# RoPE projection on one core: buffer counts, VectorE block transposes in three of four pairs, and a tail of eight single tiles

## The chip, the cores and the metric

The kernel runs on one core of one Trainium2 chip. The metric is the time of one execution on the device, in microseconds (us). The profile measures a span, from the first to the last instruction of the core; what lies around the span belongs to the time and not to the span.

## The reference

A batch of 16 sequences of 512 rows and 768 columns is multiplied by a 768 x 768 weight, and each of the 12 heads of 64 columns is rotated by its row's cosine and sine:

```python
y = np.matmul(x, weight).reshape(batch, seq, n_heads, head_dim)
y1, y2 = y[..., :32], y[..., 32:]
out1 = y1 * cos1 - y2 * sin1
out2 = y2 * cos2 + y1 * sin2
out = np.concatenate([out1, out2], axis=-1)   # float32, 16 x 512 x 768
```

## The kernel before

The 8192 rows are cut into 64 tiles of 128 rows, and the tiles into 32 pairs `n` of two tiles `s` = 0, 1 (two batches, the same rows `r`). This text numbers the tiles 2n+s, so tile 50 is the first of pair 25. A tile goes through six steps:

1. Load: `load` fetches it in one DMA of 384 KB on SP's queue into `xs` (10 buffers in `xpool`). `load_blocks` fetches a tile that `by_blocks` names in four DMAs of 96 KB into `xb` (`bpool`), each into 32 partitions with pieces of 768 bytes; the two DMAs to partitions 0 to 63 are issued by SP, the two to partitions 64 to 127 by ScalarE (ACT).
2. `cast`: ACT casts it to fp16 (`xc`, 6 buffers).
3. `transpose`: TensorE (PE) transposes it in six instructions into PSUM (`pt`, 2 buffers) and ACT copies that to `xT` (`tpool`, 9 buffers). A block tile is turned by `transpose_blocks` instead: one VectorE (DVE) instruction that transposes 32 x 32 blocks, from `xc` to `xT`.
4. `mm`: twelve matmuls into PSUM (`psy`, two buffers of three banks, a pair each).
5. `rope_pair`: DVE multiplies the pair by cosines and by sines in one instruction (`rope`, `tq`), GpSimd (POOL) adds the two halves (`add`, `ov`, 6 buffers).
6. `store`: ACT's queue writes the pair in one DMA of 768 KB, three pairs later.

The order on every engine is the program's. In the loop over the pairs, PE computes tile 2n+s, and then `upto("turn", ...)` and `upto("cast", ...)` turn and cast the tiles that are due: tile k+2 and tile k+4 after tile k in the steady part, and more from the point where the lookahead in `upto` grows, up to four tiles more, so that all transposes are done before the last `ALONE` pairs. The tiles of those pairs take their PSUM banks one by one, some of them from `pt`, and are rotated and added one by one (`rope_alone`, `add`); the very last is split between DVE and POOL (`rope_last`). `rope_pair` of the pair ahead of them runs in two halves. `load_plain(n + 5)` stands at the head of iteration n and `load_blocks(n + AHEAD_B)` at its end. Pairs 7, 9, ..., 27 have a block tile: 11 tiles. `by_blocks` and `upto` are

```python
def by_blocks(n, s):
    return s == 1 and n % 2 == 1 and 6 < n < NP - ALONE

def upto(what, k):
    k += min(4, max(0, k - 41) // 4)
```

Of the kernel before, what the change touches and what calls it, by code (L numbers as in the profile page):

```python
# [17 lines left out]
def kernel(  # L18
# [9 lines left out]
    nc = tc.nc  # L28
    P = nc.NUM_PARTITIONS

    B, S, H = x.shape
# [7 lines left out]
    NP = B * SB // 2  # L39
    CHUNKS = [(t, e) for t in range(NT) for e in range(2)]  # L40
    AHEAD = 7
    AHEAD_B = 4
    ALONE = 3

# [1 line left out]
    def where(n, s):  # L48
        return 2 * (n // SB) + s, n % SB

    def by_blocks(n, s):
        return s == 1 and n % 2 == 1 and 6 < n < NP - ALONE

    konst = ctx.enter_context(tc.tile_pool(name="konst", bufs=1))
    ident = konst.tile([P, P], FP16)
# [3 lines left out]
    w_raw = konst.tile([P, NT, 2, H], FP32)  # L59
    w_sb = konst.tile([P, NT, 2, H], FP16)  # L60

    xpool = ctx.enter_context(tc.tile_pool(name="xpool", bufs=10))
    bpool = ctx.enter_context(tc.tile_pool(name="bpool", bufs=AHEAD_B + 1))
    cpool = ctx.enter_context(tc.tile_pool(name="cpool", bufs=6))
    tpool = ctx.enter_context(tc.tile_pool(name="tpool", bufs=9))
    rpool = ctx.enter_context(tc.tile_pool(name="rpool", bufs=3))
    opool = ctx.enter_context(tc.tile_pool(name="opool", bufs=6))
    pt_pool = ctx.enter_context(tc.tile_pool(name="pt", bufs=2, space=bass.MemoryType.PSUM))
# [3 lines left out]
    xss, x16, xTT, psys, tqs, ovs = {}, {}, {}, {}, {}, {}  # L72
# [14 lines left out]
    def load_plain(n):  # L87
        for s in (0, 1):
            if n < NP and not by_blocks(n, s):
                load(n, s)  # L90


    def load_blocks(n):
        if n >= NP or not by_blocks(n, 1):
            return
        b, r = where(n, 1)
        xss[n, 1] = bpool.tile([P, H], FP32, tag="xb", name="xb")
        src = x[b].rearrange("(j a r) (q k) -> r q a j k", r=SB, a=R, q=NQ)
        dst = xss[n, 1].rearrange("p (j k) -> p j k", j=NQ)
        for q in (0, 2, 1, 3):  # L100
            eng = nc.sync if q < 2 else nc.scalar
            eng.dma_start(out=dst[ts(q, R)], in_=src[r, q])  # L102
# [9 lines left out]
    def cast(n, s, eng):  # L112
        xc = cpool.tile([P, H], FP16, tag="xc", name="xc")
        x16[n, s] = xc
        src = xss.pop((n, s))
        if by_blocks(n, s):
            src = src.rearrange("p (j a t e) -> p t (j a) e", j=NQ, t=NT, e=2)
        else:
            src = src.rearrange("p (m t e) -> p t m e", t=NT, e=2)
        copy(eng, xc.rearrange("p (t m e) -> p t m e", t=NT, e=2), src)  # L120

    def transpose(n, s, eng):
        xc = x16.pop((n, s)).rearrange("p (t m e) -> p t e m", t=NT, e=2)
        pt = pt_pool.tile([P, NT, 2, P], FP16, tag="pt", name="pt")
        for t, e in CHUNKS:
            nc.tensor.transpose(pt[:, t, e, :], xc[:, t, e, :], ident)  # L126
        xT = tpool.tile([P, NT, 2, P], FP16, tag="xT", name="xT")
        copy(eng, xT, pt)
        xTT[n, s] = xT

    def transpose_blocks(n, s):
        xT = tpool.tile([P, NT, P, 2], FP16, tag="xT", name="xT")
        nc.vector.transpose(  # L133
            out=xT.bitcast(FP32).rearrange("p t m e -> p (t m e)"),
            in_=x16.pop((n, s)).bitcast(FP32),
        )
        xTT[n, s] = xT.rearrange("p t m e -> p t e m")
# [5 lines left out]
    def psum(n, s):  # L143
        if n < NP - ALONE:
            if n not in psys:
                psys[n] = py_pool.tile([P, 3, 512], FP32, tag="psy", name="psy")
                if n < 2:
                    nc.tensor.matmul(  # L148
                        psys[n][:, 1], cold[:, 0:P], cold, start=True, stop=False
                    )  # L150
            cut = 512 if s == 0 else 256
            return [
                (psys[n][:, s, ds(s * 256, cut)], 0, cut, n < 2 and s == 1),
                (psys[n][:, s + 1, 0 : H - cut], cut, H, n < 2 and s == 0),
            ]
        if (n, s) not in psys:
            if (2 * (n - NP + ALONE) + s) % 3 == 1:
                psys[n, s] = [
                    pt_pool.tile([P, 512], FP32, tag="pt", name="psz") for _ in (0, 1)
                ]  # L160
            else:
                ps = py_pool.tile([P, 3, 512], FP32, tag="psy", name="psy")
                psys[n, s] = [ps[:, 0], ps[:, 1]]
        lo, hi = psys[n, s]
        return [(lo, 0, 512, False), (hi[:, 0 : H - 512], 512, H, False)]

    def mm(n, s, t, e):
        for ps, lo, hi, joined in psum(n, s):
            nc.tensor.matmul(  # L169
                ps,  # L170
                xTT[n, s][:, t, e, :],
                w_sb[:, t, e, lo:hi],
                start=((t, e) == CHUNKS[0] and not joined),
                stop=((t, e) == CHUNKS[-1] and not (joined and s == 0)),
            )

    def rope(n, c0, c1, ps):
        r = n % SB
        nh = (c1 - c0) // D
        if n not in tqs:  # L180
            tqs[n] = rpool.tile([P, 2, 2 * H], FP32, tag="tq", name="tq")
            ovs[n] = opool.tile([P, 2 * H], FP32, tag="ov", name="ov")
        nc.vector.tensor_tensor(  # L183
            out=tqs[n][:, :, c0:c1].rearrange("p j (h d) -> p j h d", d=D),
            in0=ps.rearrange("p (h d) -> p h d", d=D)
            .unsqueeze(1).broadcast_to((P, 2, nh, D)),
            in1=csn[:, :, r, :].unsqueeze(2).broadcast_to((P, 2, nh, D)),
            op=MULT,
        )

    def add(n, c0, c1, eng):
        w = c1 - c0
        tq = tqs[n][:, :, ds(c0, w)]
        eng.tensor_tensor(  # L194
            out=ovs[n][:, ds(c0, w)].rearrange("p (h t d) -> p h t d", t=2, d=HD),
            in0=tq[:, 0].rearrange("p (h t d) -> p h t d", t=2, d=HD),
            in1=tq[:, 1].rearrange("p (h t d) -> p h t d", t=2, d=HD)[:, :, ::-1, :],
            op=ADD,
        )

    def rope_pair(n, step=2 * H):
        ps = psys[n].rearrange("p b n -> p (b n)")
        for c in range(0, 2 * H, step):
            rope(n, c, c + step, ps[:, ds(c, step)])
            add(n, c, c + step, nc.gpsimd)

    def rope_alone(n, s):
        for ps, lo, hi, _ in psum(n, s):
            rope(n, s * H + lo, s * H + hi, ps)
# [25 lines left out]
    def store(n, eng, c0=0, c1=2 * H):  # L235
        b, r = where(n, 0)
        dst = out.rearrange("b (p r) h -> r p b h", r=SB)[r, :, b : b + 2]
        src = ovs[n].rearrange("p (b h) -> p b h", b=2)
        if c1 - c0 < 2 * H:
            s = c0 // H  # L240
            dst = dst[:, s, c0 - s * H : c1 - s * H]
            src = src[:, s, c0 - s * H : c1 - s * H]
        eng.dma_start(out=dst, in_=src)
# [21 lines left out]
    done = {"cast": 4, "turn": 4}  # L265

    def upto(what, k):
        k += min(4, max(0, k - 41) // 4)
        while done[what] < min(k, 2 * NP):
            n, s = divmod(done[what], 2)  # L270
            done[what] += 1
            if what == "cast":
                cast(n, s, nc.scalar)
            elif not by_blocks(n, s):
                transpose(n, s, nc.scalar)
# [13 lines left out]
    for k, c in enumerate(CHUNKS):  # L289
# [8 lines left out]
        out=csn[:, 1, :, HD:D], in0=sin_sb[:, :, 0:HD], scalar1=-1.0  # L298
    )
    rope_pair(0)  # L300
    upto("cast", 6)
    mm(1, 0, *CHUNKS[-1])
    upto("turn", 5)
    for c in CHUNKS:
        mm(1, 1, *c)
    upto("cast", 7)
    upto("turn", 6)
    upto("cast", 8)
    rope_pair(1)

    for n in range(2, NP):
        load_plain(n + AHEAD - 2)
        if n + 1 < NP and by_blocks(n + 1, 1):
            transpose_blocks(n + 1, 1)
        for s in (0, 1):
            for c in CHUNKS:
                mm(n, s, *c)
            upto("turn", 2 * n + s + 3)
            upto("cast", 2 * n + s + 5)
            if n >= NP - ALONE:  # L320
                if (n, s) != (NP - 1, 1):
                    rope_alone(n, s)
                    add(n, s * H, (s + 1) * H, nc.gpsimd)
        if n >= 3:
            store(n - 3, nc.scalar)
        load_blocks(n + AHEAD_B)
        if n < NP - ALONE:
            rope_pair(n, 2 * H if n < NP - ALONE - 1 else H)
    store(NP - 3, nc.scalar)
    store(NP - 2, nc.scalar)  # L330
    store(NP - 1, nc.scalar, 0, H)
    rope_last(NP - 1, 1)


# [33 lines left out]
```

## Time and profile before

| | |
|---|---|
| time, median of 5 runs | 163.8 us (163.66 to 164.43) |
| profiled execution: its own time | 165.71 us |
| profiled execution: its span | 163.9 us |
| PE busy | 150.3 us (92%) |
| DVE, POOL, ACT busy | 120.8, 110.2, 91.1 us |
| DMA | 53.17 MB, mean 324 GB/s |
| chain that ended last | PE 59%, DMA 18%, DVE 6%, POOL 5%, ACT 4% |

The profile is of one execution, whose time was 1.9 us over the median. A group's row gives its count, its busy time, the mean duration of one in ns, and the idle time of the engine before it with what ended that. PE's matmuls are pipelined, so the pitch from one group to the next in the chain of waits says more than the duration of one. In the DMA line, 9 means that the core's DMA engines were 90% or more busy.

### The profile page before, as it was taken

The numbers are of one execution on the slowest core, as the hardware profiler recorded it, in microseconds if no ns is written. First come the engines' busy times: TensorE is split into PE (matmuls) and PEld (weight loads), VectorE is DVE, ScalarE is ACT, GpSimd is POOL, SyncE is SP. The second block draws the span as 40 slices with busy tenths as digits, with TensorE's granted clock in tenths as the row PEclk, the third lists the DMA queues.
The fourth block names the chain that finished last, engine by engine and source line by source line (L and its number), as shares of the span: only waits on it lengthen the run. The fifth ranks groups of instructions, "written<-read, shape, count | busy, mean of one in ns | idle before, by whom it ended". The sixth has DMA issues, their size and how long they took to land.

```text
span 163.9 us, 2775 instructions
## 1 busy us (share of the span) xinstructions
PE 150.3 (92%) x1104; PEld 94.7 (58%) x1104; DVE 120.8 (74%) x68; ACT 91.1 (56%) x114; POOL 110.2 (67%) x40
## 2 busy tenths in 40 slices
PE   7899999999699999999999999999969799999910
PEld 2355666666366666666666666666646466666500
DVE  0556976788848787888878787879695757879970
ACT  3441866774566566765665657776193898610000
POOL 0000397777885787878788787877866774699990
PEclk9999999999999999999999999999999999999995
DMA  4999999999999999999999999999988445449766
GB/s 158 340 412 392 407 397 306 392 342 296 384 364 316 402 330 412 315 401 335 409 328 403 321 402 329 376 359 359 286 331 249 194 192 196 192 191 393 286 242 233
DMA packets 24141, 53.17 MB, mean 324 GB/s; under 512 B 2368, under 2 KB 8384, under 8 KB 24128
## 3 DMA queue, kind: packets, MB, share of 16 engines
q1 hardware_dynamic: 12096, 25.89, 47.9%
q10 hardware_dynamic: 12032, 27.10, 43.3%
q8 instruction: 8, 0.13, 0.3%
q14 instruction: 5, 0.04, 0.1%
HBM read 27.82 MB, written 25.17 MB: 323 GB/s over the span
## 4 chain that ended last, share of the span: by engine, by line
PE 59%; DMA 18%; DVE 6%; POOL 5%; ACT 4%; issue 2%; POOLq 1%; SPq 1%; ACTq 1%; DVEq 0%
PE psy L169 51%; DMA xs<-in_x_dram 10%; PE pt L126 8%; DVE tq L183 6%; POOL ov L194 5%; DMA w_raw<-in_weight_dram 4%; DMA xb<-in_x_dram 3%; ACT xT L76 2%; ACT xc L76 2%; POOLq L363 1%; SPq L83 1%; ACTq L102 1%; POOLq L194 0%; ACTq L76 0%; DVEq L183 0%
## 5 line engine op out<-in xcount | busy, mean ns | idle before, releaser
L194 POOL TENSOR_TENSOR ov<-tq 128x1536 f32<-128x1536 f32 (+2 forms) x36 | 110.0, 3065 | 49.3 <-DVE tq L183 47.7
L169 PE MATMUL psy<-w_sb,xT 128*128 128x512 f16 (+1 forms) x744 | 129.4, 326 | 1.4 <-ACT xT L76 1.2
L183 DVE TENSOR_TENSOR tq<-psy,csn 128x3072 f32<-128x3072 f32 (+3 forms) x37 | 103.4, 2808 | 29.9 <-PE psy L169 29.7
L169 PEld LDWEIGHTS <-xT 128*128 128x128 f16 x768 | 73.1, 98 | 45.7 <-ACT xT L76 1.8
L76 ACT COPY xT<-pt 128x768 f16<-128x768 f16 x51 | 40.6, 801 | 36.8 <-PE pt L126 28.5
L76 ACT CAST xc<-xs 128x768 f16<-128x768 f32 x51 | 44.8, 904 | 9.7 <-DMA xs<-in_x_dram 8.3
L126 PE MATMUL pt<-ident,xc 128*128 128x128 f16 x318 | 26.1, 220 | 3.4 <-ACT xc L76 2.7
L126 PEld LDWEIGHTS <-xc 128*128 128x128 f16 x318 | 21.8, 98 | 12.1 <-ACT xc L76 4.6
L76 ACT CAST xc<-xb 128x768 f16<-128x768 f32 x11 | 10.0, 906 | 6.7 <-DMA xb<-in_x_dram 6.7
L247 PE MATMUL cold_ps<-cold 128*128 128x512 f16 x16 | 6.2, 537 | 1.2 <-DVE cold L252 1.2
L133 DVE STREAM_TRANSPOSE xT<-xc 128x384 f32<-128x384 f32 x11 | 6.3, 568 | 0.0
L110 DVE CAST w_sb<-w_raw 128x768 f16<-128x768 f32 x6 | 3.4, 558 | 2.1 <-DMA w_raw<-in_weight_dram 2.1
L78 DVE CAST xc<-xs 128x768 f16<-128x768 f32 x2 | 1.9, 948 | 3.3 <-DMA xs<-in_x_dram 3.3
L169 PE MATMUL psz<-w_sb,xT 128*128 128x512 f16 (+1 forms) x24 | 4.2, 326 | 0.0
L247 PEld LDWEIGHTS <-cold 128*128 128x128 f16 x16 | 1.8, 126 | 3.4 <-issue 2.2
L183 DVE TENSOR_TENSOR tq<-psz,csn 128x1024 f32<-128x1024 f32 (+1 forms) x4 | 3.6, 947 | 0.0
L78 DVE COPY xT<-pt 128x768 f16<-128x768 f16 x2 | 1.1, 558 | 1.9 <-PE pt L126 1.9
L76 ACT ACT_TABLE_LOAD x1 | 1.3, 1283 | 1.1 <-PEq L349 1.1
L252 DVE MEMSET cold<- 128x256 uint32 x1 | 0.3, 272 | 0.9 <-PEq L349 0.9
L148 PE MATMUL psy<-cold 128*128 128x512 f16 x2 | 0.8, 379 | 0.0
L226 DVE TENSOR_TENSOR ov<-psy,tq 128x512 f32<-128x512 f32 x1 | 0.7, 692 | 0.0
L222 DVE TENSOR_TENSOR psy<-psy,csn 128x512 f32<-128x512 f32 x1 | 0.7, 689 | 0.0
(8 smaller groups left out, 1.7 us busy)
## 6 DMA issues: line engine op xcount, KB each, us to landing
out_dram<-ov ACTq DMA_DIRECT2D x31, 768.0 KB, 6.6
xs<-in_x_dram SPq DMA_DIRECT2D x53, 384.0 KB, 6.6
w_raw<-in_weight_dram SPq DMA_DIRECT2D x6, 384.0 KB, 7.6
xb<-in_x_dram SPq DMA_DIRECT2D x22, 96.0 KB, 6.5
xb<-in_x_dram ACTq DMA_DIRECT2D x22, 96.0 KB, 6.1
out_dram<-ov ACTq DMA_DIRECT2D x1, 384.0 KB, 3.4
out_dram<-ov SPq DMA_DIRECT2D x1, 256.0 KB, 2.4
csn<-in_cos_dram SPq DMA_DIRECT2D x1, 128.0 KB, 7.8
```

Of the source, the lines that this page charges most:

```text
L76: eng.copy(out=o, in_=i_)
L78: eng.tensor_copy(out=o, in_=i_)
L83: nc.sync.dma_start(out=xss[n, s], in_=x[b].rearrange("(p r) h -> r p h", r=SB)[r])
L102: eng.dma_start(out=dst[ts(q, R)], in_=src[r, q])
L110: nc.vector.tensor_copy(out=w_sb[:, t, e], in_=w_raw[:, t, e])
L126: nc.tensor.transpose(pt[:, t, e, :], xc[:, t, e, :], ident)
L133: nc.vector.transpose(out=xT.bitcast(FP32).rearrange("p t m e -> p (t m e)"), in_=x16.pop((n, s)).bitcast(FP32),)
L169: nc.tensor.matmul(ps, xTT[n, s][:, t, e, :], w_sb[:, t, e, lo:hi], start=((t, e) == CHUNKS[0] and not joined), stop=((t, e) == CHUNKS[-1] ...
L183: nc.vector.tensor_tensor(out=tqs[n][:, :, c0:c1].rearrange("p j (h d) -> p j h d", d=D), in0=ps.rearrange("p (h d) -> p h d", d=D) .unsqu ...
L194: eng.tensor_tensor(out=ovs[n][:, ds(c0, w)].rearrange("p (h t d) -> p h t d", t=2, d=HD), in0=tq[:, 0].rearrange("p (h t d) -> p h t d", ...
L247: nc.tensor.matmul(cold_ps, cold[:, 0:P], cold, start=True, stop=True)
L363: with _tile.TileContext(nc) as tc:
```

## The change

- `ALONE` goes from 3 to 4: the last eight tiles, not six, are handled alone, and each is stored by itself as soon as it is added. The pair ahead of them is rotated in one piece.
- `by_blocks` names the second tile of three pairs in four, from pair 7 to 27: 16 tiles.
- `AHEAD_B` goes from 4 to 6, `bpool` from 5 to 7 buffers; a `load_blocks(7)` is put before the loop.
- `xpool` goes from 10 to 7 buffers, `tpool` from 9 to 11.
- The lookahead in `upto` begins 10 tiles earlier and grows to six tiles.
- In the loop, the store of pair n-3 stands after `load_blocks`, and the stores of the last three pairs that are stored whole come at the end of iteration 27.

```diff
-    AHEAD_B = 4
-    ALONE = 3
+    AHEAD_B = 6
+    ALONE = 4
...
-        return s == 1 and n % 2 == 1 and 6 < n < NP - ALONE
+        return s == 1 and n % 4 > 0 and 6 < n < NP - ALONE
...
-    xpool = ctx.enter_context(tc.tile_pool(name="xpool", bufs=10))
+    xpool = ctx.enter_context(tc.tile_pool(name="xpool", bufs=7))
...
-    tpool = ctx.enter_context(tc.tile_pool(name="tpool", bufs=9))
+    tpool = ctx.enter_context(tc.tile_pool(name="tpool", bufs=11))
...
-    def rope_pair(n, step=2 * H):
-        ps = psys[n].rearrange("p b n -> p (b n)")
-        for c in range(0, 2 * H, step):
-            rope(n, c, c + step, ps[:, ds(c, step)])
-            add(n, c, c + step, nc.gpsimd)
+    def rope_pair(n):
+        rope(n, 0, 2 * H, psys[n].rearrange("p b n -> p (b n)"))
+        add(n, 0, 2 * H, nc.gpsimd)
...
-        k += min(4, max(0, k - 41) // 4)
+        k += min(6, max(0, k - 31) // 4)
...
+    load_blocks(7)
     for n in range(2, NP):
...
                     rope_alone(n, s)
                     add(n, s * H, (s + 1) * H, nc.gpsimd)
-        if n >= 3:
-            store(n - 3, nc.scalar)
+                    store(n, nc.scalar, s * H, (s + 1) * H)
         load_blocks(n + AHEAD_B)
         if n < NP - ALONE:
-            rope_pair(n, 2 * H if n < NP - ALONE - 1 else H)
-    store(NP - 3, nc.scalar)
-    store(NP - 2, nc.scalar)
-    store(NP - 1, nc.scalar, 0, H)
+            if n >= 3:
+                store(n - 3, nc.scalar)
+            rope_pair(n)
+        if n == NP - ALONE - 1:
+            for m in (n - 2, n - 1, n):
+                store(m, nc.scalar)
     rope_last(NP - 1, 1)
```

## The prediction

> **What bounds the kernel now.** I read the page's busy times, then the chain of waits, then the timeline where the chain leaves PE, then a table of stretches one pair long. The chain first:
>
> ```profile
> 47.66 0.34 PE pt L126 x6
> 48.00 1.95 PE psy L169 x12
> 49.95 0.34 PE pt L126 x6
> 50.28 3.90 PE psy L169 x24
> 54.18 0.33 PE pt L126 x6
> ```
>
> From 16.7 to 107 us the chain is PE alone but for one break: a tile's twelve matmuls take 1.95 us, six transposes 0.34 us, and after a block tile's place there are 24 matmuls in a row. So PE sets the pace, and 64 x 1.95 + 53 x 0.34 = 143 us of the span is its plain work. The rest is the start, a few stalls and the tail. The stalls, from the timeline:
>
> ```profile
> 43.25 2.12 PE L169 MATMUL psy<-w_sb,xT 128*128 128x512 f16 x12 [1.25 <-ACT xT L76]
> ...
> 111.94 0.86 ACTq L102 DMA_DIRECT2D xb<-in_x_dram  x2
> ...
> 118.97 0.90 ACT L76 CAST xc<-xb 128x768 f16<-128x768 f32 x1 [3.73 <-DMA xb<-in_x_dram]
> ...
> 122.12 0.51 PE L126 MATMUL pt<-ident,xc 128*128 128x128 f16 x6 [1.40 <-ACT xc L76]
> ...
> 127.58 0.89 ACT L76 CAST xc<-xb 128x768 f16<-128x768 f32 x1 [2.96 <-DMA xb<-in_x_dram]
> ...
> 130.02 0.51 PE L126 MATMUL pt<-ident,xc 128*128 128x128 f16 x6 [0.87 <-ACT xc L76]
> ```
>
> PE stalls 1.25 + 1.40 + 0.87 = 3.5 us after the start. The last two have one cause: ACT's half of a block tile's load is issued only some 7 us before its cast (111.94 to 118.97), a landing takes 6.1 us in the median, and when the lookahead begins to grow the cast comes due earlier than the load. The plain loads are not late: in the DMA queue's waits SP waits 36.0 us, 19 times, for an ACT cast to free an `xs` buffer.
>
> DMA is the second bound. Stretches of 4.4 us, one pair each, with the DMA share and GB/s last:
>
> ```profile
> 56.00:60.40 4.40, 4.40 (x37) 2.96 (x36) 3.83 (x2) 2.19 (x4) 3.64 (x2) 1.00 1.03 328
> 60.40:64.80 4.40, 4.40 (x33) 2.71 (x32) 3.38 (x2) 3.39 (x5) 3.29 (x2) 1.00 1.04 409
> 64.80:69.20 4.40, 4.40 (x37) 2.97 (x36) 3.82 (x2) 2.62 (x5) 3.62 (x2) 1.00 1.05 324
> 69.20:73.60 4.40, 4.40 (x33) 2.73 (x32) 3.38 (x2) 2.96 (x4) 3.29 (x2) 1.00 1.04 402
> ```
>
> The share is full throughout, and every second pair, where a block tile's load is in flight, moves about 326 GB/s instead of 405. That is 4.4 x (1 - 326/405) = 0.86 us of DMA capacity lost for each block tile. A plain tile of 393,216 bytes takes 0.97 us at 405 GB/s.
>
> **What the Trainium skill says.** SBUF — State Buffer, section "Door 1: The DMA port swizzle", maps partitions 0 to 63 to only eight of sixteen DMA ports; SP's two block DMAs both go there. The dips above agree with it, but nothing here separates the port from the smaller pieces. DMA: Bandwidth & Descriptors, section "Issuing engines are not separate DMA queues", says that SP's and ACT's DMAs share the same 16 engines: more block DMAs take capacity from plain loads and stores alike. Its section "Specifications" has an HBM limit of about 358 GB/s per core; the 409 above is more, so I use the measured rate. VectorE: DVE Perf Modes, section "The three transpose paths", says that DVE transposes 32 x 32 blocks independently, which is why the load has to place the blocks; the trace has 0.57 us for one such instruction.
>
> **The change part by part.**
>
> Five more block tiles. PE loses 5 x 6 transposes: 5 x 0.335 = **-1.7 us**, on the path. ACT loses five copies of 0.80 us, hidden (it is 56% busy). DVE gains 5 x 0.57 us: a pair with a block tile lasts 3.90 + 0.34 = 4.24 us on PE, and 3.36 + 0.57 = 3.93 fits. If that cover were gone, a rotation would start 0.3 to 0.6 us late and the matmuls two pairs on would wait for `psy`. DMA loses 5 x 0.86 = 4.3 us more of its capacity. DMA issues: `xb` 44 to 64 (half on SP, half on ACT), `xs` 53 to 48.
>
> Block loads two pairs earlier (`AHEAD_B`, `bpool`, `load_blocks(7)`). In the steady part ACT's half is issued four pairs before its cast, about 17 us against 6.1 to 10 us for a landing. With the new lookahead the shortest lead, by counting iterations, is pair 27: issued at the end of iteration 21, cast after tile 46, 1.5 pairs or 6.4 us; pairs 25 and 26 have two pairs, 8.6 us. So the 1.40 and 0.87 us should go. The 1.25 us at 43 came after ACT sat until 41.6 us on the issue of a block load; ACT now issues three such pairs in four, so I let that stay or recur.
>
> Fewer `xs`, more lookahead. A plain tile may be fetched seven plain tiles ahead, 11 tiles or 24 us at 2.16 us a tile (ten were 13 tiles): still over three times a landing, no cost in the steady part. The lookahead asks for more loads earlier, and that meets the DMA. Check it at the end of tile 50, where PE needs tile 58 turned, so 59 tiles loaded. PE without a stall gets there at about 123.5 us: it began tile 58 at 144.4; minus 3.5 of stalls, 1.7 of transposes and two tiles of 1.95 gives 135.3 for tile 56, minus five tiles and six turns. DMA by then: first data at 1.8 us; 59 tiles, 6.7 tiles' worth of weight and tables, and 42 stored tiles (pairs 0 to 20): 107.7 x 0.97 = 104.5; 16 block tiles x 0.86 = 13.8; an estimated 1.5 idle while seven buffers throttle the early loads; 2.3 for the last landing and its cast. Sum 123.9: as late as PE. A low bound of 0.8 for a block tile gives 123.0. For the upper end I use the page's slices 3 to 29, which average 362 GB/s: 11.7 us lost in 110.6, or 1.1 each over 11 tiles, which gives 127.7. So the DMA wait lies between 0 and 4.2 us; I take 1.5, somewhat over the sum, since arrivals come in bursts.
>
> ACT's queue. Ten DMA issues in four pairs instead of eight can hold casts and copies behind them; the list of waits has 5.2 us of such holds in 4 places, none of which reached PE. Between 0 and 2 us more; I take 1.1 with the stall at 43 in it. Moving the store behind `load_blocks` alters nothing else: it was ready a pair before.
>
> The tail. Before, from the start of tile 58:
>
> ```profile
> 143.22 16.55 POOL L194 TENSOR_TENSOR ov<-tq 128x1536 f32<-128x1536 f32 x9 [1.45 <-DVE tq L183]
> ...
> 144.35 5.15 DVE L183 TENSOR_TENSOR tq<-psy,csn 128x1536 f32<-128x1536 f32 x4 [1.21 <-PE psy L169]
> ```
>
> POOL is never idle from 143.2 to 159.8, 15.4 us after tile 58 began, and PE ends at 156.2: the tail hangs on POOL. After, from the start of tile 56: rotation of pair 27 in one piece, 3.4; its add 3.46; seven tiles at POOL's pitch of 1.77, 12.4; the last piece 0.8: 20.1 us. Before, the same stretch was 2 x 1.95 + 15.4 = 19.3. So **+0.7 us**, because pair 27's add starts a rotation later. The bounds are 0 and 1. The single stores cost nothing: the last two tiles were stored singly before, and at the end the DMA is half empty.
>
> Sum against the profiled span: -1.7 + 0.7 - 3.5 + (1.5 + 1.1) = **-1.9 us**: 163.9 to 162.0. That execution was 1.9 us over the median of the runs, and some of its stalls may be its own; I take the same difference from the median, 163.8 - 1.9 = **161.9 us**.
>
> **The rivals.**
>
> *DMA becomes the bound* (slower). Four pairs move 16 tiles, 15.5 us, and three block tiles, 2.6 to 3.3: 18.1 to 18.8 us, while PE needs 17.3. Before it was 15.5 + 1.7 = 17.2 against 17.6. SP also waits 23.4 us, 13 times, for a store to land, though no load needs one; I read that as a limit on the DMAs in flight, and quarter loads would fill it. If that or too thin a stock of early loads starves the casts, PE waits in pairs 18 to 26. It decides once PE's stalls pass 3.5 + 1.0 = 4.5 us. At 1.2 us a block tile plus 1.5 us of holds, stalls are about 6: 165.3 us. For it: the share of 1.03 to 1.05 now. Against: SP still waits for buffers, not for data.
>
> *All stalls go* (faster): -1.7 + 0.7 - 3.5 = -4.5, so 159.3 to 160.3 us. For it: both late stalls have one cause, which the earlier load takes away. Against: the full DMA share.
>
> *The stall moves* (no change): ACT, held by DMA issues while the lookahead makes it 1.25 times as busy, stalls PE by 3.5 to 5 us: 163.3 to 164.3 us.
>
> That the edits do not take hold, for want of slots, would also be no change; the pools only differ in count, so I give it nothing of its own.
>
> **How the numbers follow.** Forecast 0.50, all stalls gone 0.12, the stall moves 0.14, DMA bound 0.24. A measurement of this kernel tells about 0.3% (0.5 us) from no change. Faster: 0.62, same 0.14, slower 0.24. The range, 159.9 to 165.2, takes in the forecast's own range (160.0 to 163.2, stalls of 0.7 to 3.9 us), the whole of the moved stall and most of the other two.
>
> **What would show it.** Right: 48 sets of turns, no ACT wait of over 1 us for `xb`, POOL without a gap in the last 16 us, PE stalls of 2 to 3 us in all. Wrong: SP waiting mainly for DMAs instead of casts and ACT waiting for `xs` between 90 and 125 us (DMA bound); PE waiting for `xT` or `xc` behind ACT's issues with data long landed (the stall moved); a tail over 20.5 us from tile 56 to POOL's end.

## The result, and the profile after

| | before | after |
|---|---|---|
| ratio after : before, 95% interval | | 1.0005 [0.9984, 1.0027] |
| median of all runs | 164.43 us (77 runs) | 166.35 us (42 runs) |
| fastest to slowest run | 162.75 to 166.44 | 162.70 to 168.71 |
| profiled execution: time, span | 165.71, 163.9 us | 166.97, 165.2 us |
| PE, DVE, ACT busy | 150.3, 120.8, 91.1 us | 149.3, 123.6, 87.0 us |

No change. The ratio is formed from the runs within 1.5% of each kernel's fastest, which is why it is lower than the medians of all runs suggest (by those, after is 1.2% longer). 161.9 us was forecast; the rival that the stall moves is what happened.

The page of after first, its busy times:

```profile
PE 149.3 (90%) x1074; PEld 93.0 (56%) x1074; DVE 123.6 (75%) x75; ACT 87.0 (53%) x109; POOL 110.2 (67%) x40
```

and from its groups (count, busy time and mean ns, idle time before and its releaser) and its list of DMA issues:

```profile
L169 PE MATMUL psy<-w_sb,xT 128*128 128x512 f16 (+1 forms) x732 | 127.0, 326 | 4.4 <-ACT xT L76 4.2
...
L126 PE MATMUL pt<-ident,xc 128*128 128x128 f16 x288 | 23.9, 221 | 3.0 <-ACT xc L76 2.5
...
L133 DVE STREAM_TRANSPOSE xT<-xc 128x384 f32<-128x384 f32 x16 | 9.1, 569 | 0.7 <-ACT xc L76 0.7
...
out_dram<-ov ACTq DMA_DIRECT2D x7, 384.0 KB, 2.3
```

The edit took hold: 288 transposes are 48 sets of six, and 16 tiles are turned on DVE. But PE, with less work, is idle more: it waits for ACT's copies and casts. The timeline of after has each stall since the start, in the last bracket:

```profile
39.64 2.12 PE L169 MATMUL psy<-w_sb,xT 128*128 128x512 f16 x12 [1.55 <-ACT xT L76]
...
54.77 2.12 PE L169 MATMUL psy<-w_sb,xT 128*128 128x512 f16 x12 [1.70 <-ACT xT L76]
...
90.80 4.07 PE L169 MATMUL psy<-w_sb,xT 128*128 128x512 f16 x24 [0.94 <-ACT xT L76]
...
103.65 0.51 PE L126 MATMUL pt<-ident,xc 128*128 128x128 f16 x6 [1.93 <-ACT xc L76]
```

They sum to 6.1 us, against 3.5 before. The two late stalls of before, at 122 and 130 us, are gone; four others stand in their place. What ACT did ahead of the first, on ACT's timeline of after (ACTq rows are DMA issues):

```profile
34.19 0.32 ACTq L102 DMA_DIRECT2D xb<-in_x_dram  x1
...
35.70 0.32 ACTq L102 DMA_DIRECT2D xb<-in_x_dram  x1
38.33 0.41 ACTq L241 DMA_DIRECT2D out_dram<-ov  x1
38.79 0.80 ACT L76 COPY xT<-pt 128x768 f16<-128x768 f16 x1 [3.63 <-DMA xb<-in_x_dram]
```

ACT is idle for 3.63 us ahead of the copy at 38.79, though that reads only `pt`, which PE's transposes of 35.30 us had filled by 35.8. What holds it stands ahead of it in ACT's program: the block load issued at 35.70 and the store issued at 38.33. The other three stalls follow such issues too, at 53.44, 89.06 and 89.49, and 101.57 us. Their waits can be read from the semaphores in the trace. Each DMA issued by SP or ACT counts its landing on one of eight semaphores, taken in turn in one order that runs over both queues, and its issue waits until the DMA that last had that semaphore, eight DMAs earlier, has landed. From the trace's records, in us:

```
engine, what      issued   eight earlier landed   in flight just before
ACT  xb load      34.19    34.17                  7
SP   xb load      34.76    34.74                  7
ACT  xb load      35.70    35.68                  7
SP   xb load      35.85    35.83                  7
SP   xs load      38.05    37.99                  7
ACT  store        38.33    38.26                  7
SP   xs load      38.70    38.64                  7
SP   xs load      40.41    40.15                  7
ACT  xb load      40.83    40.81                  7
```

So at most eight DMAs of SP and ACT are in flight, each for the 6 to 7 us that a landing takes. Over the whole execution, of the 150 issues that have such a predecessor none came before its landing, and 79 came within 0.12 us after it; in the kernel before it was 45 of 132. SP can stand in such a wait, it computes nothing. ACT can't: the copies and casts behind it stand too. The waits of after give the size (total, times, longest):

```profile
ACT xT L76 <- DMA xb<-in_x_dram: 15.6, 5, 4.4
...
PE psy L169 <- ACT xT L76: 4.2, 3, 1.7
```

The data themselves were early: by the records, the load of pair 9's block tile had landed at 35.8 us and was cast at 49.6. After 25 us no cast of a plain tile came less than 4 us after its data had landed, and no cast of a block tile less than 1.1 us.

The tail of after, on the timeline. PE begins the matmuls of tile 56 at 142.17 us, just after it hands pair 27 to DVE:

```profile
142.11 5.09 DVE L183 TENSOR_TENSOR tq<-psy,csn 128x3072 f32<-128x3072 f32 x3 [1.21 <-PE psy L169]
...
145.55 16.54 POOL L194 TENSOR_TENSOR ov<-tq 128x1536 f32<-128x1536 f32 x9 [1.12 <-DVE tq L183]
```

POOL ends at 162.09 us, 19.9 us after tile 56 began, and the span 3.1 us later.

### The profile page after: what moved, and what is told of

Its sections match the earlier page's. It is cut to its first block, busy times and chain, and to the rows that moved or that the text cites. A ratio compares the mean times of both kernels' runs of the same rounds, so it can differ in the third digit from the quotient of the medians.

```text
span 165.2 us, 2741 instructions
## 1 busy us (share of the span) xinstructions
PE 149.3 (90%) x1074; PEld 93.0 (56%) x1074; DVE 123.6 (75%) x75; ACT 87.0 (53%) x109; POOL 110.2 (67%) x40
## 2 busy tenths in 40 slices
DMA packets 26349, 53.17 MB, mean 322 GB/s; under 512 B 2656, under 2 KB 11232, under 8 KB 26336
## 4 chain that ended last, share of the span: by engine, by line
PE 33%; POOL 32%; issue 12%; DVE 10%; DMA 8%; POOLq 1%; ACT 1%; SPq 1%; ACTq 0%; DVEq 0%
POOL ov L194 32%; PE psy L169 28%; DVE tq L183 10%; PE pt L126 5%; DMA w_raw<-in_weight_dram 4%; DMA xs<-in_x_dram 4%; ACT xc L76 1%; POOLq L363 1%; SPq L83 1%; POOLq L194 0%; ACT xT L76 0%; ACTq L241 0%; DVEq L183 0%
## 5 line engine op out<-in xcount | busy, mean ns | idle before, releaser
L169 PE MATMUL psy<-w_sb,xT 128*128 128x512 f16 (+1 forms) x732 | 127.0, 326 | 4.4 <-ACT xT L76 4.2
L183 DVE TENSOR_TENSOR tq<-psy,csn 128x3072 f32<-128x3072 f32 (+2 forms) x38 | 102.9, 2724 | 27.6 <-PE psy L169 27.4
L76 ACT COPY xT<-pt 128x768 f16<-128x768 f16 x46 | 36.6, 801 | 44.0 <-PE pt L126 24.3
L76 ACT CAST xc<-xs 128x768 f16<-128x768 f32 x46 | 41.0, 904 | 9.6 <-DMA xs<-in_x_dram 8.5
L126 PE MATMUL pt<-ident,xc 128*128 128x128 f16 x288 | 23.9, 221 | 3.0 <-ACT xc L76 2.5
L126 PEld LDWEIGHTS <-xc 128*128 128x128 f16 x288 | 19.8, 99 | 11.2 <-ACT xc L76 4.0
L76 ACT CAST xc<-xb 128x768 f16<-128x768 f32 x16 | 14.5, 906 | 1.4 <-DMA xs<-in_x_dram 1.4
L133 DVE STREAM_TRANSPOSE xT<-xc 128x384 f32<-128x384 f32 x16 | 9.1, 569 | 0.7 <-ACT xc L76 0.7
L169 PE MATMUL psz<-w_sb,xT 128*128 128x512 f16 (+1 forms) x36 | 6.3, 326 | 0.0
L183 DVE TENSOR_TENSOR tq<-psz,csn 128x512 f32<-128x512 f32 (+1 forms) x5 | 4.3, 898 | 0.1
```

The source lines that it names most:

```text
L76: eng.copy(out=o, in_=i_)
L133: nc.vector.transpose(out=xT.bitcast(FP32).rearrange("p t m e -> p (t m e)"), in_=x16.pop((n, s)).bitcast(FP32),)
L169: nc.tensor.matmul(ps, xTT[n, s][:, t, e, :], w_sb[:, t, e, lo:hi], start=((t, e) == CHUNKS[0] and not joined), stop=((t, e) == CHUNKS[-1] ...
L183: nc.vector.tensor_tensor(out=tqs[n][:, :, c0:c1].rearrange("p j (h d) -> p j h d", d=D), in0=ps.rearrange("p (h d) -> p h d", d=D) .unsqu ...
```

## The experiments

Ratios are against the kernel before, from runs on the same chip. Theory 1: ACT is held by its DMA issues, which wait for a place among the eight. Theory 2: DMA capacity, or the way the block loads use it, is the bound. Where an edit is made on the kernel before, it says so; the others are made on after. The expectations name some of the versions by numbers: e1 is the first one below, with all block loads on SP, e2 the one with the tail's pair in two halves, e3 the kernel before with early block loads, and e5 the one with the loop's stores on POOL's queue.

### All block loads on SP

```diff
-            eng = nc.sync if q < 2 else nc.scalar
+            eng = nc.sync
```

> The changed kernel with all four block DMAs of a tile issued by SP, none by ACT. Theory 1 (ACT's queue is held while a block DMA waits to be issued, and PE waits for the copies and casts behind it): PE's stalls after the start fall from 6.1 us to about 2, the waits of ACT's copies for a block DMA (15.6 us) go, time 0.975 to 0.985 of the kernel before. Theory 2 (DMA capacity is the bound): the same bytes in the same pieces over the same engines, so the time stays at about 1.000 and PE's stalls only change their place.

Measured: 1.0003 [0.9972, 1.0035], median 165.73 us. On the waits, ACT's row for block loads is gone and PE has no stall before 97 us; then 1.38, 1.93 and 0.45 us, at 97, 113 and 122 us. The list of SP's waits shows why:

```profile
SPq L102 <- DMA out_dram<-ov: 23.2, 11, 5.7
SPq L83 <- DMA out_dram<-ov: 10.5, 6, 4.9
```

The loads, on L102 and L83, need no store, and wait 33.7 us for stores to land: with the block loads ahead of them in SP's order and stores among the eight, the plain loads now come late, and ACT's casts wait for `xs` data, 20.6 us in 8 places, of which 8.2 us are at the start, before 16 us. The hold went, and the time didn't: by its number this is theory 2's outcome, and theory 1's 0.975 to 0.985 failed. The waits say that the limit moved from ACT to SP; whether this or DMA capacity sets the time is decided by the later experiments.

### The pair ahead of the tail in two halves

```diff
-            rope_pair(n)
+            if n < NP - ALONE - 1:
+                rope_pair(n)
+            else:
+                for c in (0, H):
+                    rope(n, c, c + H, psys[n].rearrange("p b n -> p (b n)")[:, ds(c, H)])
+                    add(n, c, c + H, nc.gpsimd)
```

> The changed kernel with the rotation and add of pair 27 in two halves again. If POOL's chain sets the end, it starts its last stretch half a rotation earlier and the time falls by 0.7 to 1.3 us, to 0.992 to 0.996 of the kernel before. If the end is set elsewhere, no change from 1.000. It says nothing on theories 1 and 2 on the middle.

Measured: 1.0011 [0.9976, 1.0046], 166.5 us. From tile 56 to POOL's end took 18.9 us instead of 19.9, as costed; but ACT's holds grew to 18.0 us and PE's stalls to 7.3 us in the profiled execution. Inconclusive on the time: the stalls scatter more than the 1 us sought.

### The kernel before, with the block loads two pairs earlier

```diff
-    AHEAD_B = 4
+    AHEAD_B = 6
...
+    load_blocks(7)
     for n in range(2, NP):
```

> The kernel before with its 11 block tiles loaded six pairs ahead instead of four, and nothing else. Theory 1: ACT's half of a block tile is no longer late, so the stalls of 1.40 and 0.87 us near 122 and 130 us go; ACT has no more DMA issues than before, so no new holds: time 0.986 to 0.992. Theory 2: the bytes are the same and the DMA share was full, so 0.997 to 1.003.

Measured: 1.0112 [1.0076, 1.0149], 167.49 us. The two late stalls are gone, as predicted for this edit, and one larger one appears. ACT's timeline and then PE's:

```profile
41.00 3.63 ACTq L102 DMA_DIRECT2D xb<-in_x_dram  x2
44.67 0.80 ACT L76 COPY xT<-pt 128x768 f16<-128x768 f16 x1 [5.58 <-DMA xs<-in_x_dram]
```

```profile
45.53 2.83 PE L169 MATMUL psy<-w_sb,xT 128*128 128x512 f16 x12 [3.84 <-ACT xT L76]
```

and stretches of it, with PE's busy time first, the granted clock third from the end, then DMA share and GB/s:

```profile
40.00:45.50 5.50, 1.69 (x11) 0.78 (x8) 4.43 (x3) 0.83 (x2) 3.70 (x2) 1.00 0.99 370
45.50:50.00 4.50, 4.47 (x22) 2.65 (x23) 0.00 (x0) 2.52 (x4) 3.18 (x1) 0.64 1.06 313
50.00:54.50 4.50, 4.50 (x37) 2.97 (x36) 2.79 (x1) 2.22 (x3) 0.00 (x0) 0.98 1.04 389
```

With no more block tiles and no more DMA issues than before, ACT is held 5.58 us in front of a copy; by the records each of the two block loads ahead of it was issued 0.02 us after the DMA eight before it had landed. Neither theory's number held: theory 1 had expected no new hold. Then the clock falls. The Trainium skill, TensorE: Matmul & The Clock Gate, section "Part 1: The HAM clock gate (the "warmup" mystery)", says that the clock drops to half after an idle window of about 3.4 us. This agrees: after 3.84 us idle the grant was 0.64 over 4.5 us (by the clock records, half from 46.8 to 50.2 us, which is 1.3 us after PE had resumed), while after the 1.55 us stall of after, in the stretch 39.6 to 41.8 us, it was 1.00. So this stall was paid for again, by an estimate from the grant: 4.5 x (1 - 0.64) = 1.6 us.

### Both edits on the kernel before: early, and all block loads on SP

```diff
-    AHEAD_B = 4
+    AHEAD_B = 6
...
-            eng = nc.sync if q < 2 else nc.scalar
+            eng = nc.sync
...
+    load_blocks(7)
```

> The kernel before with its 11 block tiles loaded six pairs ahead (as in e3) and all their DMAs on SP. Theory 1: e3's stall of 3.84 us at 45 us was ACT held at the issue of a block DMA, so it goes, and the two late stalls stay away as in e3: PE without a stall of 0.5 us, time 0.977 to 0.985. Theory 2: the same bytes at a full share, 0.997 to 1.003.

Measured: 0.9805 [0.9762, 0.9849], 161.5 us, one stall of 0.24 us. It differs from the last kernel by one line, which engine issues half of the block loads, and is 3.0% faster (0.9805 / 1.0112), as theory 1 had it. The pages of that kernel and of this one show the same packets:

```profile
DMA packets 24141, 53.17 MB, mean 322 GB/s; under 512 B 2368, under 2 KB 8384, under 8 KB 24128
```

```profile
DMA packets 24141, 53.17 MB, mean 331 GB/s; under 512 B 2368, under 2 KB 8384, under 8 KB 24128
```

Over 40 to 120 us the DMA share was 1.03 in both. So with the same DMAs at the same share, the engine that issues them decides. With 11 block tiles SP can carry them, though its loads still wait 18.8 us for stores; with 16, in the first experiment, it couldn't as long as the stores shared the eight.

### Block loads over all partitions

```diff
-        for q in (0, 2, 1, 3):
-            eng = nc.sync if q < 2 else nc.scalar
-            eng.dma_start(out=dst[ts(q, R)], in_=src[r, q])
+        for j in (0, 2, 1, 3):
+            eng = nc.sync if j < 2 else nc.scalar
+            eng.dma_start(out=dst[:, j], in_=src[r, :, :, j])
```

> The changed kernel with each of the four block DMAs cut by rows instead of by columns: each writes all 128 partitions, still 512 pieces of 768 bytes per tile, still two on SP and two on ACT. If the dips in the DMA rate come from writing only 32 partitions at a time, pairs with a block load rise from about 330 GB/s to about 400 and landings get shorter; by theory 2 the time then falls to 0.975 to 0.985. By theory 1 ACT is still held at each issue, a little shorter since landings come sooner: 0.990 to 1.000. If the dips come from the pieces of 768 bytes, the rate stays and so does the time.

Measured: 1.2282 [1.2225, 1.2338], 202.58 us: the opposite. Stretches of it:

```profile
56.00:60.40 4.40, 2.15 (x16) 1.12 (x13) 3.67 (x3) 0.00 (x0) 3.27 (x1) 0.99 0.28 109
60.40:64.80 4.40, 1.44 (x5) 0.74 (x6) 1.22 (x1) 2.29 (x3) 3.27 (x2) 0.50 0.82 281
64.80:69.20 4.40, 4.40 (x26) 2.45 (x24) 0.58 (x1) 0.56 (x2) 0.33 (x1) 0.74 0.54 179
```

The DMA engines are busy 28 to 82% and move 109 to 281 GB/s. The Trainium skill, DMA: Bandwidth & Descriptors, section "Why a DMA increments its semaphore by 16 and not by 1", says that a DMA issued by SP or ACT uses as many engines as the largest number up to 16 that divides the slowest dimension of both sides. Here that of the source is 4, so by an estimate from this rule four engines instead of sixteen. The low share fits; which engines carried these loads was not read. With loads this slow among the eight, ACT's holds reached 39.2 us. This says nothing on the swizzle of ports that it was meant for.

### Block loads on SP, and the loop's stores on POOL's queue

```diff
-            eng = nc.sync if q < 2 else nc.scalar
+            eng = nc.sync
...
-                store(n - 3, nc.scalar)
+                store(n - 3, nc.gpsimd)
```

> All four block DMAs on SP, as in e1, and the stores of whole pairs inside the loop issued by POOL instead of ACT. Theory 1, restated after e1 (a load's issue waits until the DMA eight before it in a common order has landed; on ACT that holds copies, on SP it makes plain loads late because a store stands eight before): loads no longer wait for stores, SP's waits for out_dram go, PE's stalls fall below 1 us, time 0.975 to 0.985 of the kernel before, less if POOL's issue of a DMA delays its adds. Theory 2 (DMA capacity): the same bytes and pieces, 0.997 to 1.003.

Measured: 0.9687 [0.9644, 0.9731], 159.62 us, span 157.8, below theory 1's range. PE has no stall after 17 us. SP's waits of this kernel:

```profile
SPq L102 <- DMA xs<-in_x_dram: 23.7, 20, 2.1
SPq L83 <- ACT xc L76: 13.4, 15, 3.5
```

and a stretch of 80 us (its length, then PE; clock, DMA share and GB/s last), of this kernel and then of after:

```profile
40.00:120.00 80.00, 80.00 (x593) 51.48 (x591) 67.85 (x33) 53.95 (x68) 75.02 (x38) 1.00 1.03 367
```

```profile
40.00:120.00 80.00, 75.40 (x557) 47.77 (x555) 61.75 (x31) 50.63 (x65) 57.40 (x18) 1.00 1.04 355
```

No load waits for a store any more. The trace's records show POOL's stores on semaphores of their own and 7 to 9 DMAs in flight at most issues, where it was at most 7 in after. The same bytes, at a DMA share of 1.03, feed a PE that is never idle from 40 to 120 us. The loads' pieces are the same; the stores' are not, since the page counts 23,150 packets against 26,349 in after. That this isn't the cause is shown by the pair of kernels above, which have the same packets, and by the version with the stores alone on POOL below, which has the packets of this one and is slower. A full share therefore wasn't a bound, and theory 2 falls; theory 1 stands in a wider form: what counts is which loads wait for a place among the eight, and which engine carries the waiting issue. SP's issues still wait so, 23.7 us in the first line, but nothing behind them is late. POOL pays 0.73 us an issue, between its adds, and its adds stay at 3.46 us.

### The lookahead later, with block loads on SP

```diff
-            eng = nc.sync if q < 2 else nc.scalar
+            eng = nc.sync
...
-        k += min(6, max(0, k - 31) // 4)
+        k += min(6, max(0, k - 37) // 4)
```

> All four block DMAs on SP, as in e1, and the lookahead begins six tiles later, at k = 37 in place of 31. In e1 PE's stalls of 1.38, 1.93 and 0.45 us lie at 97 to 122 us, while the lookahead grows. If casts ask for plain loads before these can have come, six tiles of delay are 13 us more of time for them: stalls of 1 to 2 us, time 0.987 to 0.994. If the supply lags by rate (theory 2), the stalls come later but stay: 0.997 to 1.003.

Measured: 1.0276 [1.022, 1.0331], 169.29 us. In the lookahead the stalls fell from 3.8 to 2.1 us, but the edit made a new one of 5.43 us at 145 us: the turns weren't finished when the tail needs the banks of `pt`. Neither forecast held, and how much of the stalls is the lookahead's can't be read from this time.

### One plain DMA for a block tile

```diff
-        for q in (0, 2, 1, 3):
-            eng = nc.sync if q < 2 else nc.scalar
-            eng.dma_start(out=dst[ts(q, R)], in_=src[r, q])
+        nc.sync.dma_start(
+            out=xss[n, 1], in_=x[b].rearrange("(p r) h -> r p h", r=SB)[r]
+        )
```

> The changed kernel with each block tile fetched by one plain DMA of 384 KB on SP; the columns are then not in the order that the block transpose needs, so the data of these tiles is another. 110 DMAs instead of 158. Both theories: no stall after the start, about 0.972 to 0.982. Theory 2 adds that every pair then moves 390 GB/s or more while the DMA share is full; by theory 1 the share itself falls under 1.0, since DMA had capacity left. If the time stays at 1.00, both fall.

This version leaves out the placing of the blocks, so it measures time and is no replacement. Measured: 0.9671 [0.9632, 0.971], 159.45 us. No stall after the start, with the stores still on ACT's queue. SP's waits:

```profile
SPq L83 <- ACT xc L76: 74.2, 33, 5.2
```

After the start SP's loads wait for buffers almost alone, which is how one wants it. With one place of the eight instead of four for a block tile, the limit no longer binds. That it gets no faster than the stores on POOL, though its loads are cheaper for the DMA (it moved 378 GB/s over the 80 us), says again that capacity wasn't what the time hung on. What each theory added did not come true: stretches of one pair moved 355 to 415 GB/s, not all of them 390, and the share over the 80 us was 1.00, not under it.

### The stores alone moved to POOL

```diff
-                store(n - 3, nc.scalar)
+                store(n - 3, nc.gpsimd)
```

> The changed kernel with only the loop's stores moved to POOL; half of each block tile's DMAs stay on ACT. If the hold of ACT needs the stores among the eight DMAs in flight, the holds go and the time is that of e5, 0.966 to 0.974. If loads alone fill the eight, ACT is still held at a block DMA: stalls of 2 to 5 us, 0.980 to 1.000.

Measured: 0.9844 [0.9775, 0.9913], median 163.8 us, with single runs from 160.9 to 165.22. The profiled execution is the shortest of the six, 160.9 us: ACT still has half of the block loads and is held 7.0 us in 2 places; PE has one stall of 1.00 us. What the longer runs stalled was not profiled. Each half alone is worth less than the two: block loads off ACT nothing, both 3.1%, and here every run is longer than all six of the version with both. The size of this half is open: 1.6% by the ratio, 0.3% by the medians.

### Eleven block tiles in the good version

```diff
-        return s == 1 and n % 4 > 0 and 6 < n < NP - ALONE
+        return s == 1 and n % 2 == 1 and 6 < n < NP - ALONE
...
-            eng = nc.sync if q < 2 else nc.scalar
+            eng = nc.sync
...
-                store(n - 3, nc.scalar)
+                store(n - 3, nc.gpsimd)
```

> e5 with 10 or 11 block tiles (every second pair, as before the change) instead of 16. PE has five or six more sets of six transposes at 0.335 us, now with no stall to hide in: 1.7 to 2.0 us over e5, 0.979 to 0.982 of the kernel before. If DMA set the pace of e5, fewer block tiles cost nothing: 0.967 to 0.972.

Measured: 0.981 [0.9776, 0.9843], 161.22 us, no stall. Against the same kernel with 16 block tiles, 159.62 us: 1.6 us by the medians, 2.0 us by the ratios (1.2% of 164), which are taken on two chips. The five tiles are worth what they were priced at once nothing stalls.

### Ten buffers

```diff
-    xpool = ctx.enter_context(tc.tile_pool(name="xpool", bufs=7))
+    xpool = ctx.enter_context(tc.tile_pool(name="xpool", bufs=10))
```

> The changed kernel with ten xs buffers again instead of seven. The prediction gave the smaller number no cost in the steady part: 0.997 to 1.003, with the same stalls at ACT's issues. If seven buffers throttle SP so that its loads crowd with ACT's, ten bring loads forward and PE's stalls fall by 1 to 3 us: 0.98 to 0.995. If SP running ahead fills the eight DMAs in flight, as a rival to both, ACT is held longer: 1.005 to 1.02.

Measured: 1.033 [1.0265, 1.0395], 172.15 us. More buffers make it slower. PE's timeline of the profiled execution, of 173.31 us, has among five stalls of 10.5 us in all

```profile
45.88 2.12 PE L169 MATMUL psy<-w_sb,xT 128*128 128x512 f16 x12 [2.62 <-ACT xT L76]
...
59.28 4.02 PE L169 MATMUL psy<-w_sb,xT 128*128 128x512 f16 x12 [4.42 <-ACT xT L76]
```

With more room SP runs further ahead: from 50 to 120 us plain data had landed 20 to 30 us before their cast, against 11 to 18 in after. The holds on ACT's copies are 21.1 us (13.4 that ended with the landing of a block load and 7.7 with that of a plain one) against 17.0 in after (15.6 and 1.4). That SP's loads, being earlier, keep the places from ACT fits this; it was not shown by itself. At the stall of 4.42 us the clock fell to 0.50, from 58.0 to 64.8 us.

### The good version with the tail's pair in halves

The edits of "Block loads on SP, and the loop's stores on POOL's queue" and of "The pair ahead of the tail in two halves" together.

> e5 (block DMAs on SP, loop stores on POOL) with the rotation and add of pair 27 in two halves, as in e2. Without stalls before it, the tail is measured by itself: POOL's last stretch starts 1.1 to 1.7 us earlier and ends 0.7 to 1.3 us earlier, so 0.960 to 0.966 of the kernel before, against 0.9687 of e5. If the stores or DVE set the end, as in e5, 0.966 to 0.971.

Measured: 0.9697 [0.9666, 0.9729], 159.4 us, less than the expected gain: the interval overlaps that without the halves. From tile 56 to POOL's end took 19.6 us, 0.3 less, not 1. In the version without the halves POOL stands idle only 0.45 us ahead of pair 27's add, since its store issue of 0.73 us lies there; there was little more to gain. This and the version without are the fastest that keep the rearranged loads, 3.0 to 3.1% faster than before.

## Why the prediction was wrong, point by point

**Five more block tiles, -1.7 us: right.** 48 sets of turns, no stall from DVE, and 1.6 to 2.0 us between 11 and 16 block tiles in a kernel without stalls.

**The late stalls of 1.40 and 0.87 us go: right.** They are gone in after, and in the kernel before with that edit alone.

**The tail, +0.7 us: right in its path, and a term was missed at its end.** From tile 56 to POOL's end 20.1 us was worked out, 19.9 measured. But from POOL's end to the span's end is 3.1 us, where it was 4.1: stores of 384 KB, issued one by one while the DMA is little more than half busy (5 to 6 tenths in the page's last three slices), land in 2.3 us. The single stores "cost nothing" should have been a gain of 1 us.

**"Fewer `xs` ... no cost in the steady part": right as far as it went, wrong in what it looked for.** Seven buffers don't starve anything; ten in their place cost 3.2% more. The pool's size also sets how far SP runs ahead, and in the version with ten ACT's holds were longer.

**DMA wait, 1.5 us: wrong.** The ledger of DMA capacity gave 123.9 us for DMA's arrival at tile 50 and set it against PE's 123.5. With the stores on POOL PE waited for nothing, at the same bytes and share. The term is 0, and the rival built on it (165.3 us) had a mechanism that does not decide here. That rival did name the limit on DMAs in flight, as something that would starve the casts; the limit was real, and the queue it hurts first is ACT's.

**ACT's queue, 1.1 us: this is the step that failed.** "Between 0 and 2 us more" was carried over from before, with its 5.2 us of holds, "none of which reached PE". In the profiled execution all 6.1 us of stalls stand behind ACT and no part behind data: 6.1 us where 1.1 was put. And one hold of before did reach PE. The list of waits has it under another name, but ACT's timeline of before shows it ahead of PE's stall at 43.25 us, which the prediction had itself put down to the issue of a block load:

```profile
41.19 1.16 ACTq L102 DMA_DIRECT2D xb<-in_x_dram  x2
42.40 0.80 ACT L76 COPY xT<-pt 128x768 f16<-128x768 f16 x1 [2.98 <-PE psy L169]
```

The transposes that this copy reads had ended at 40.06 us, and by the records the issue at 41.19 came 0.02 us after its predecessor's landing. So the wait that stalls after was in before already, 1.25 us of it on the path. The count of issues, ten in four pairs instead of eight, was the wrong measure: with the count unchanged and the block loads merely earlier, the kernel before was 1.1% slower. An issue costs 0.32 to 0.41 us, a full set of eight costs the time until a landing, and held ACT up to 4.4 us. More evidence was in the waits of before, SP's 13 for a store that no load needs:

```profile
SPq L83 <- DMA out_dram<-ov: 23.4, 13, 4.1
```

The prediction read it as a limit on DMAs in flight and then used it only for SP. The Trainium skill, DMA: Bandwidth & Descriptors, section "Issuing engines are not separate DMA queues", says that issuing from several engines only saves issue time; here the choice of engine for half of the block loads moved the time by 3.0%, since an issue also waits and holds what is behind it. The measurement decides. Of the rivals, the moved stall named this mechanism; its range of 163.3 us on belongs to stalls of 4 us, and its own 3.5 us would have begun it at 162.8.

The sum with the measured terms, for the two profiled spans (their executions took 1.3 and 0.6 us more than the medians of all runs): -1.7 (turns) + 0.7 (tail) - 1.0 (last stores) + 2.6 (stalls, 6.1 - 3.5) + 0.3 (the first steady transposes start at 17.01 instead of 16.70 us) = +0.9 us; the spans differ by +1.3. The 0.4 us left is not placed. With the stalls at zero, the same sum is -1.7 + 0.7 - 1.0 - 3.5 = -5.5 us; the version with block loads on SP and the loop's stores on POOL gave 3.1% of 164.4, which is 5.1 us, and 6.1 us by its profiled span. The gain that the change holds is there, and was lost to a wait that had stalled PE once before the change and stalled it four times after.

What stays open: why the stalls vary between runs. After's times spread over 6.0 us, those of the four versions without a stall over 0.6 to 0.8 us in six runs each, which fits stalls that depend on which landing comes first; it was not traced run by run. It is open too why the halved clock came when it did, and it was not tried whether the hardware would take more than eight: the eight are the semaphores that this program waits on.

## What to carry to other kernels

Before pricing an added DMA, find what its issue waits for: count how many are in flight at each issue, and where that number stands still and issues follow a landing at once, the issue waits for that landing, and everything behind it on that engine with it. So put DMA issues that may wait on an engine that computes nothing, or on one with slack and landing semaphores of its own, and use few large DMAs where the places are limited. A wait for a DMA that the waiting instruction doesn't need, as of a load for a store, is the sign to look for. It isn't yet a loss: with 11 block tiles all on SP, loads waited 18.8 us for stores and PE stalled 0.24 us. And more buffers can make it worse.

## What the runs showed that was not expected

- Loads cut to cover all 128 partitions with a source of four outer rows ran at 109 to 281 GB/s in the stretches shown, against 290 to 410 for after's in stretches of that length from 56 to 82 us, and cost 23% of the time.
- A PE stall of 3.84 us was followed by 4.5 us at a granted clock of 0.64; with one of 4.42 us it was 0.50 for 6.8 us.
- A pair's store issued by POOL takes 0.73 us of POOL's time, against 0.41 us on ACT, and left POOL's adds at 3.46 us.
- Three more input buffers in after cost 3.2%: 1.033 against 1.0005.
